# Feed-forward on one core: one pair of plain column blocks instead of two, and token sums formed just ahead of the block products that use them

## The chip, the cores and the metric

The kernel runs on one core of one Trainium2 chip. The metric is the device time of one launch in microseconds (us); of the kernel before three runs are shown, and their median is what the changed kernel is held against. The engines are named as in the profile: PE (TensorE, matmuls), PEld (its weight loads), DVE (VectorE), ACT (ScalarE), POOL (GpSimd), SP (SyncE, which here issues DMAs).

## The reference, cut to what matters

A trunk of two layers over 512 tokens of width 1024, in float32. Each layer has a feed-forward, a token mixer (layer 0: attention beside a gated delta rule; layer 1: a state-space scan) and another feed-forward, so there are four feed-forwards in all. The change touches these alone:

```
def swiglu(x, w_gate, w_up, w_down):
    return (jax.nn.silu(x @ w_gate) * (x @ w_up)) @ w_down
...
        f = swiglu(rmsnorm(h, nw[0]), ffn_w_gate[layer, 0], ffn_w_up[layer, 0], ffn_w_down[layer, 0])
        h = h + FFN_RES_SCALE * rmsnorm(f, nw[1])
```

`w_gate` and `w_up` are 1024 x 2816, that is 22 column blocks of 128.

## The kernel before, in words

**Float32 products as three matmuls.** Each operand is split into a high part `hi` (a cast on ACT, line 80) and a rest `lo` (a subtraction on DVE, line 81); a product is hi·hi + hi·lo + lo·hi. The normalised tokens stand transposed in two tiles `uhi` and `ulo` (together `uT`: 4 token blocks x 8 blocks of the contraction x 128). A unit of weights is 128 x 1024 numbers (512 KB): it is loaded into a raw tile (`wraw`, 3 buffers, or `wq`, 5 buffers) and split into `whi` and `wlo` (4 buffers each, for all of the kernel).

**The order of the columns in a feed-forward** (`ffn`, lines 304 to 438). Blocks are done in pairs.

1. Blocks 0 and 1 (`early`, lines 326 to 336): gate and up of both, four units, which hold all four `whi`/`wlo` buffers. Every product is done for token blocks 0 and 1 first, then for 2 and 3 (24 matmuls of 256 columns each time), since the last tokens come late from the stage before. Then `finish` (lines 320 to 323) takes SiLU of the gate on ACT and multiplies it with the up product on DVE into a tile `hT`.
2. Blocks 2 and 3 (`plain`, lines 338 to 344): four products of 24 matmuls over all 512 tokens.
3. Token sums (lines 347 to 370): with `uT` seen as a 2 x 2 matrix of quarters A11, A12 (first tokens) and A21, A22 (last tokens), the full-precision quarters r11, r12, r21, r22 are formed (hi + lo, line 352) and combined into S2, S1n, S3 and S4, each again split into hi and lo (`parts`). The r tiles are four of the eleven buffers that `place` gives out under the name `h`, and the `hT` tiles come from the same eleven. S4 is written over A21.
4. Blocks 4 to 21, nine pairs (lines 392 to 423): gate and up of a pair together take seven block products (`block_product`, line 293) of 24 matmuls with 256 columns, by Winograd's scheme: b11·A11, b21·A12, (t1 + b22)·S2, t1·S1n, t3·S3, b22·S4, (b11 + b21)·A22, the sums on the weights' side among them. A pair loads seven units: five by SP, and two more by POOL as loads that add into a `wq` tile already there (line 380: t1 and t3). The sum b11 = t1 + b22 (line 405) waits for the first of these and for b22.

Then `out_product` multiplies with `w_down` and applies the norms, the residual and the next norm (`finish` and `pre` there), and the transposed tokens of the next stage come out of it, token block by token block.

**What sets the order.** The text gives each instruction a priority, its place in the program. When the kernel is built, every engine gets one list: of what is ready by the builder's model of times, the earliest in the text goes first. On the chip each engine runs its list in that order. `self.tc.cur_priority` (lines 148 and 157) moves the transposes of the last tokens back by a count of instructions (`BEHIND`). Buffers of one name are given out in the order in which the text first writes them.

**A count that spans stages.** `weights` counts units in `n_weights` (line 93), and in the even mixer, where `share` is set, every fifth has its `lo` formed by POOL instead of DVE (line 94). A `w_cols` or `w_rows` unit counts, a `unit`/`forms` of the block pairs doesn't.

Of the kernel before, what the change touches and what calls it, by code (L numbers as in the profile page):

```python
# [14 lines left out]
OP = mybir.AluOpType  # L15
# [15 lines left out]
class Trunk:  # L31
# [272 lines left out]
    def ffn(self, w_gate, w_up, w_down, post_w, next_pre, raws={}):  # L304
# [3 lines left out]
        nf = w_gate.shape[1] // 128  # L308
        tt, stt = nc.vector.tensor_tensor, nc.vector.scalar_tensor_tensor
        with ExitStack() as ctx:  # L310
            hp = ctx.enter_context(self.tc.tile_pool(name="ffn_h", bufs=1, reuse_waits="tile"))

            place = lambda dt=F32: hp.tile([128, 2, T], dt, name="h", bufs=nf // 2)
            early, plain = 2, 2
            acc, wts, hT = {}, {}, []
            with ExitStack() as ctx2:
                pool = lambda name, **kw: ctx2.enter_context(self.tc.tile_pool(name=name, reuse_waits="tile", **kw))
# [2 lines left out]
                def finish(f):  # L320
                    s = self.scratch()
                    nc.scalar.activation(s, acc[f, 0], AF.Silu)
                    tt(hT[f // 2][:, f % 2, :], acc[f, 1], s, op=OP.mult)

                r11, r12, r21, r22 = (place().rearrange("p f (k c) -> p f k c", c=128) for _ in range(4))
                for f in range(early):
                    for g, w in ((0, w_gate), (1, w_up)):
                        wts[f, g] = self.w_cols(w, f * 128, raw=raws.get((f, g)))
                        acc[f, g] = self.ps("acc" if f else "mm")
                        self.product(acc[f, g][:, :256], wts[f, g], 0, 2)  # L330
                for f in range(early):
                    for g in range(2):
                        self.product(acc[f, g][:, 256:], wts[f, g], 2, 4)
                    if f == 0:
                        hT.append(place())
                    finish(f)

                for f in range(early, early + plain):
                    if f % 2 == 0:
                        hT.append(place())  # L340
                    for g, w in ((0, w_gate), (1, w_up)):
                        acc[f, g] = self.ps("mm")
                        self.product(acc[f, g], self.w_cols(w, f * 128))
                    finish(f)


                half = lambda i, j: [u[:, 2 * i:2 * i + 2, 4 * j:4 * j + 4, :] for u in self.uT]
                A11, A12, A21, A22 = (half(i, j) for i in range(2) for j in range(2))
                flat = lambda x: x.rearrange("p t k c -> p t (k c)")

                def whole(r, x):
                    tt(flat(r), flat(x[0]).bitcast(F32), flat(x[1]).bitcast(F32), op=OP.add)

                def parts(r, x):
                    self.split(flat(r), *(flat(y) for y in x))
                    return x

                new = lambda n: [sp.tile([128, 2, KD // 2, 128], F32R, name=n + x) for x in ("hi", "lo")]
                whole(r11, A11)
                whole(r21, A21)  # L360
                whole(r22, A22)
                tt(flat(r21), flat(r22), flat(r21), op=OP.subtract)
                stt(flat(r11), flat(r21), -1.0, flat(r11), op0=OP.mult, op1=OP.subtract)
                S2 = parts(r11, new("s2"))
                S1n = parts(r21, new("s1"))
                stt(flat(r22), flat(r11), -1.0, flat(r22), op0=OP.mult, op1=OP.subtract)
                S3 = parts(r22, new("s3"))
                whole(r12, A12)
                stt(flat(r12), flat(r11), -1.0, flat(r12), op0=OP.mult, op1=OP.subtract)
                S4 = parts(r12, A21)  # L370

                def unit(f, pool, name, *parts):

                    raw = pool.tile([128, KD // 2, 256], F32, name=name)
                    for i, (w, k) in enumerate(parts):
                        src = w[k * 128:(k + KD // 2) * 128, f * 128:(f + 2) * 128].rearrange("(k p) c -> p k c", p=128)
                        if i == 0:
                            nc.sync.dma_start(raw, src)
                        else:
                            nc.gpsimd.dma_start(raw, src, accum_op=OP.add)  # L380
                    return raw

                def forms(raw):
                    hi, lo = (self.wsplit.tile([128, KD // 2, 256], F32R, name=x) for x in ("whi", "wlo"))
                    self.split(raw, hi, lo)
                    return hi, lo
# [2 lines left out]
                q = lambda n: qp.tile([128, 512], F32, name=n)  # L389

                two = lambda x: x.rearrange("p (f t) -> p f t", f=2)
                for f in range(early + plain, nf, 2):
                    b11, b21 = unit(f, wq, "wq", (w_gate, 0)), unit(f, self.wraw, "wraw", (w_gate, 4))
                    t1 = unit(f, wq, "wq", (w_gate, 0), (w_up, 0))
                    b22 = unit(f, self.wraw, "wraw", (w_up, 4))
                    t3 = unit(f, wq, "wq", (w_up, 4), (w_up, 0))
                    a = self.ps("mm")
                    self.block_product(a, forms(b11), A11, True)
                    q1 = q("q1")
                    nc.scalar.copy(q1, a)  # L400
                    c = self.ps("acc")
                    self.block_product(c, forms(b21), A12, True)
                    add(q1, c, q1)
                    nc.scalar.activation(q1, q1, AF.Silu)
                    add(b11, t1, b22)
                    self.block_product(a, forms(b11), S2, False)
                    q2 = q("q2")
                    nc.scalar.copy(q2, a)
                    d = self.ps("acc")
                    self.block_product(d, forms(t1), S1n, True)  # L410
                    q3 = q("q3")
                    nc.scalar.copy(q3, d)
                    self.block_product(a, forms(t3), S3, False)
                    add(q3, a, q3)
                    self.block_product(d, forms(b22), S4, False)
                    add(q2, d, q2)
                    hT.append(place())
                    stt(hT[-1][:, :, :256], two(q2), -1.0, two(q1), op0=OP.mult, op1=OP.mult)
                    add(b21, b11, b21)
                    self.block_product(a, forms(b21), A22, False)  # L420
                    s = self.scratch()
                    nc.scalar.activation(s, a, AF.Silu)
                    stt(hT[-1][:, :, 256:], two(q3), -1.0, two(s), op0=OP.mult, op1=OP.mult)
# [778 lines left out]
```

## Time and profile before

| | us |
|---|---|
| Runs of the kernel before | 2155.16, 2157.08, 2158.19 |
| Their median | 2157.08 |
| The profiled execution, its own time | 2155.31 |
| Its span, first to last instruction | 2153.5 |
| PE busy in the span | 2112.7 |
| DVE busy in the span | 1479.1 |
| ACT busy in the span | 1026.2 |

Durations come from the one profiled execution, so a sum stands against its own time; 1.8 us of that lie outside the span. The granted clock of PE was 0.996 of its full 2.4 GHz as a mean over the span. The matmuls overlap one another, so that the distance from one start to the next, not the duration, says what a matmul takes.

### The profile page before, as it was taken

To read this page: it belongs to the slowest core of one execution; us is meant where nothing else is said; L and a number is where in the kernel's file an instruction comes from. 1 tells how busy PE (TensorE), PEld (TensorE's weight loads), DVE (VectorE), ACT (ScalarE), POOL (GpSimd) and SP (SyncE) were. 2 spreads that over 40 slices of the span, in tenths; PEclk is the share of its full clock that TensorE was granted. 3 is DMA by queue.
4 is the path that set the end of the run, shared out by engine and by line. 5 is a ranking of instruction groups with operands and counts; after the bars stand their busy time and mean duration, and the time that the engine had idled before them with its cause. 6 is when DMAs were issued, how large, how long until landed. Compare 5 with 4: busy or idle time off the path is not lost.

```text
span 2153.5 us, 33163 instructions
## 1 busy us (share of the span) xinstructions
PE 2112.7 (98%) x13311; PEld 1871.1 (87%) x13311; DVE 1479.1 (69%) x2329; ACT 1026.2 (48%) x1577; POOL 149.5 (7%) x142
## 2 busy tenths in 40 slices
PE   8999999999999999999999999999999999999998
PEld 7999988887788999988899998877778788999986
DVE  5866656869667767656686765668888846867653
ACT  4544543455563454534344455347565423544541
POOL 0011000111200011000001100000000000011000
PEclk9999999999999999999999999999999999999999
DMA  8687334342323687533658642324334236586321
GB/s 235 148 195 167 118 100 135 101 126 66 88 70 117 158 205 176 127 118 98 157 138 196 157 132 94 101 74 118 98 90 126 69 118 157 142 196 157 122 89 68
DMA packets 284037, 277.06 MB, mean 129 GB/s; under 512 B 18576, under 2 KB 244552, under 8 KB 283884
## 3 DMA queue, kind: packets, MB, share of 16 engines
q1 hardware_dynamic: 243308, 228.81, 35.0%
q0 software_dynamic: 40576, 46.14, 13.0%
q8 instruction: 104, 1.70, 0.3%
q14 instruction: 49, 0.40, 0.1%
HBM read 265.93 MB, written 4.79 MB: 126 GB/s over the span
## 4 chain that ended last, share of the span: by engine, by line
PE 84%; DVE 7%; DMA 4%; ACT 3%; issue 1%; SPq 0%; POOL 0%; DVEq 0%; ACTq 0%; POOLq 0%
PE mm L300 18%; PE acc L300 13%; PE acc L235 9%; PE acc L237 9%; PE acc L236 9%; PE mm L169 4%; PE mm L168 4%; PE mm L167 4%; DMA wraw<-in_ffn_w_up_dram 2%; DMA M<-rows_o 1%; PE acc L649 1%; DVE wlo L81 1%; PE tr L154 1%; PE acc L169 1%; PE acc L167 1%
## 5 line engine op out<-in xcount | busy, mean ns | idle before, releaser
L80 ACT CAST whi<-wraw 128x1024 fp32r<-128x1024 f32 x296 | 310.0, 1049 | 400.0 <-PE acc L237 107.4
L81 DVE TENSOR_TENSOR wlo<-wraw,whi 128x1024 fp32r<-128x1024 f32 x292 | 356.5, 1223 | 143.4 <-ACT whi L80 141.6
L167 PE MATMUL mm<-uhi,whi 128*128 128x512 f32 (+1 forms) x736 | 274.1, 373 | 1.6 <-DVE feat L476 1.3
L168 PE MATMUL mm<-ulo,whi 128*128 128x512 f32 (+1 forms) x736 | 272.9, 371 | 0.2 <-DVE ulo L81 0.2
L169 PE MATMUL mm<-uhi,wlo 128*128 128x512 f32 (+1 forms) x736 | 271.5, 369 | 0.0
L80 ACT CAST whi<-wq 128x1024 fp32r<-128x1024 f32 x144 | 150.8, 1049 | 241.4 <-issue 77.4
L81 DVE TENSOR_TENSOR wlo<-wq,whi 128x1024 fp32r<-128x1024 f32 x144 | 175.4, 1222 | 96.7 <-ACT whi L80 96.6
L235 PE MATMUL acc<-whi,hs 128*128 128x512 f32 x576 | 227.3, 395 | 0.0
L236 PE MATMUL acc<-wlo,hs 128*128 128x512 f32 x576 | 227.2, 394 | 0.0
L380 POOL DMA_DIRECT2D wq<-in_ffn_w_up_dram x72 | 92.7, 1290 | 1074.3 <-DMA wq<-in_ffn_w_gate_dram 404.0
L300 PE MATMUL mm<-uhi,whi 128*128 128x256 f32 x576 | 163.8, 284 | 3.2 <-DVE q L388 3.1
L300 PE MATMUL mm<-uhi,wlo 128*128 128x256 f32 x576 | 163.0, 283 | 0.0
L300 PE MATMUL mm<-ulo,whi 128*128 128x256 f32 x576 | 163.0, 283 | 0.0
L300 PE MATMUL acc<-uhi,whi 128*128 128x256 f32 x576 | 162.8, 283 | 0.0
L300 PE MATMUL acc<-uhi,wlo 128*128 128x256 f32 x576 | 162.8, 283 | 0.0
L300 PE MATMUL acc<-ulo,whi 128*128 128x256 f32 x576 | 162.8, 283 | 0.0
L167 PEld LDWEIGHTS mm<-uhi,whi 128*128 128x128 f32 x736 | 139.1, 189 | 26.3 <-issue 2.9
L168 PEld LDWEIGHTS mm<-ulo,whi 128*128 128x128 f32 x736 | 139.4, 189 | 25.2 <-issue 5.0
L169 PEld LDWEIGHTS mm<-uhi,wlo 128*128 128x128 f32 x736 | 139.4, 189 | 23.8 <-issue 3.6
L237 PE MATMUL acc<-whi,hs 128*128 128x512 f32 x384 | 151.5, 395 | 0.0
L236 PEld LDWEIGHTS acc<-wlo,hs 128*128 128x128 f32 x576 | 108.5, 188 | 25.3
L235 PEld LDWEIGHTS acc<-whi,hs 128*128 128x128 f32 x576 | 108.5, 188 | 25.0
(393 smaller groups left out, 5240.1 us busy)
## 6 DMA issues: line engine op xcount, KB each, us to landing
wraw<-in_ffn_w_down_dram SPq DMA_DIRECT2D x88, 512.0 KB, 3.5
wq<-in_ffn_w_gate_dram SPq DMA_DIRECT2D x72, 512.0 KB, 5.4
wq<-in_ffn_w_up_dram POOLq DMA_DIRECT2D x72, 512.0 KB, 7.6
wraw<-in_ffn_w_gate_dram SPq DMA_DIRECT2D x52, 512.0 KB, 5.4
wraw<-in_ffn_w_up_dram SPq DMA_DIRECT2D x52, 512.0 KB, 6.4
wraw<-in_odd_w_in_dram SPq DMA_DIRECT2D x40, 512.0 KB, 3.9
wq<-in_ffn_w_up_dram SPq DMA_DIRECT2D x36, 512.0 KB, 3.8
wraw<-in_even_w_in_dram SPq DMA_DIRECT2D x28, 512.0 KB, 4.3
```

Source lines behind the costliest of these rows:

```text
L80: nc.scalar.copy(hi, src)
L81: (nc.gpsimd if on_pool else nc.vector).tensor_tensor(lo, src, hi.bitcast(F32), op=OP.subtract)
L154: nc.tensor.transpose(p[:, j * 128:(j + 1) * 128], u[:, k * 128:(k + 1) * 128], self.ident)
L167: nc.tensor.matmul(p, whi[:, k, :], hi, start=k == 0, stop=False)
L168: nc.tensor.matmul(p, whi[:, k, :], lo, start=False, stop=False)
L169: nc.tensor.matmul(p, wlo[:, k, :], hi, start=False, stop=k == KD - 1)
L235: nc.tensor.matmul(p, ahi, hi, start=k == 0, stop=False)
L236: nc.tensor.matmul(p, ahi, lo, start=False, stop=False)
L237: nc.tensor.matmul(p, alo, hi, start=False, stop=k == nk - 1)
L300: self.nc.tensor.matmul(p[:, f * 256:(f + 1) * 256].rearrange("p (t c) -> p t c", c=128), l, r, start=new and f == k == i == 0, stop=f == ...
L380: nc.gpsimd.dma_start(raw, src, accum_op=OP.add)
L649: nc.tensor.matmul(p[:, c, :], lhs[:, c, :], rhs[:, c, :], start=True, stop=True)
```

## The change

The second plain pair (blocks 2 and 3) goes; its columns become a tenth block pair, at the front of the loop. The loop over block pairs starts right behind `early`. r11 and r12 are formed between the first and second halves of the early products. The other sums are formed in the first block pair, each by `token_sum(n)` behind the split of the weights and just ahead of the block product that takes it.

```diff
-            early, plain = 2, 2
+            early = 2
...
+                whole(r11, A11)
+                whole(r12, A12)
                 for f in range(early):
                     for g in range(2):
                         self.product(acc[f, g][:, 256:], wts[f, g], 2, 4)
...
-                for f in range(early, early + plain):
-                    if f % 2 == 0:
-                        hT.append(place())
-                    for g, w in ((0, w_gate), (1, w_up)):
-                        acc[f, g] = self.ps("mm")
-                        self.product(acc[f, g], self.w_cols(w, f * 128))
-                    finish(f)
...
-                whole(r11, A11)
-                whole(r21, A21)
-                whole(r22, A22)
-                tt(flat(r21), flat(r22), flat(r21), op=OP.subtract)
-                stt(flat(r11), flat(r21), -1.0, flat(r11), op0=OP.mult, op1=OP.subtract)
-                S2 = parts(r11, new("s2"))
-                S1n = parts(r21, new("s1"))
-                stt(flat(r22), flat(r11), -1.0, flat(r22), op0=OP.mult, op1=OP.subtract)
-                S3 = parts(r22, new("s3"))
-                whole(r12, A12)
-                stt(flat(r12), flat(r11), -1.0, flat(r12), op0=OP.mult, op1=OP.subtract)
-                S4 = parts(r12, A21)
+                sums = {}
+
+                def token_sum(n):
+
+                    if n in sums:
+                        return sums[n]
+                    if n == 2:
+                        whole(r21, A21)
+                        whole(r22, A22)
+                        tt(flat(r21), flat(r22), flat(r21), op=OP.subtract)
+                        stt(flat(r11), flat(r21), -1.0, flat(r11), op0=OP.mult, op1=OP.subtract)
+                        sums[n] = parts(r11, new("s2"))
+                    elif n == 1:
+                        sums[n] = parts(r21, new("s1"))
+                    elif n == 3:
+                        stt(flat(r22), flat(r11), -1.0, flat(r22), op0=OP.mult, op1=OP.subtract)
+                        sums[n] = parts(r22, new("s3"))
+                    else:
+                        stt(flat(r12), flat(r11), -1.0, flat(r12), op0=OP.mult, op1=OP.subtract)
+                        sums[n] = parts(r12, A21)
+                    return sums[n]
...
-                for f in range(early + plain, nf, 2):
+                for f in range(early, nf, 2):
...
-                    self.block_product(a, forms(b11), S2, False)
+                    wt, u = forms(b11), token_sum(2)
+                    self.block_product(a, wt, u, False)
...
-                    self.block_product(d, forms(t1), S1n, True)
+                    wt, u = forms(t1), token_sum(1)
+                    self.block_product(d, wt, u, True)
...
-                    self.block_product(a, forms(t3), S3, False)
+                    wt, u = forms(t3), token_sum(3)
+                    self.block_product(a, wt, u, False)
...
-                    self.block_product(d, forms(b22), S4, False)
+                    wt, u = forms(b22), token_sum(4)
+                    self.block_product(d, wt, u, False)
```

## Rows read from the trace of the kernel before

**Rows 1.** The page: busy time by engine, and the chain that ended last by engine

```profile
PE 2112.7 (98%) x13311; PEld 1871.1 (87%) x13311; DVE 1479.1 (69%) x2329; ACT 1026.2 (48%) x1577; POOL 149.5 (7%) x142
...
PE 84%; DVE 7%; DMA 4%; ACT 3%; issue 1%; SPq 0%; POOL 0%; DVEq 0%; ACTq 0%; POOLq 0%
```

**Rows 2.** Stretches: length, busy PE, PEld, DVE, ACT, POOL, granted clock, DMA, GB/s

```profile
41.55:63.34 21.79, 21.79 (x98) 18.03 (x97) 14.97 (x14) 7.19 (x8) 0.00 (x0) 1.00 0.34 91
63.34:243.80 180.46, 180.46 (x1513) 180.45 (x1512) 130.64 (x132) 93.39 (x113) 19.29 (x15) 1.00 0.69 167
700.98:712.48 11.50, 11.50 (x96) 11.31 (x95) 5.37 (x6) 5.73 (x7) 2.62 (x2) 1.00 0.93 233
...
1086.45:1270.70 184.25, 181.69 (x1513) 180.65 (x1512) 130.11 (x132) 93.28 (x113) 19.28 (x15) 1.00 0.68 163
```

**Rows 3.** The chain that ended last, two block pairs of the first feed-forward

```profile
80.67 5.76 PE mm L300 x48
...
100.72 5.76 PE mm L300 x48
```

**Rows 4.** DVE in order of time, first feed-forward, from the second halves to the sums

```profile
34.12 1.23 DVE L81 TENSOR_TENSOR wlo<-wraw,whi 128x1024 fp32r<-128x1024 f32 x1 [5.64 <-ACT whi L80]
36.05 0.69 DVE L323 TENSOR_TENSOR h<-mm,scr 128x512 f32<-128x512 f32 x1 [0.71 <-ACT scr L322]
...
42.25 0.69 DVE L323 TENSOR_TENSOR h<-acc,scr 128x512 f32<-128x512 f32 x1 [1.19 <-PE acc L169]
...
52.73 0.69 DVE L323 TENSOR_TENSOR h<-mm,scr 128x512 f32<-128x512 f32 x1 [2.17 <-PE mm L169]
53.34 4.62 DVE L352 TENSOR_TENSOR h<-uhi,ulo 128x1024 f32<-128x1024 f32 x4
```

**Rows 5.** DVE in order of time, second feed-forward

```profile
690.16 0.15 DVE L106 TENSOR_SCALAR rs_x<-ss_sum 128x1 f32<-128x1 f32 x1
690.22 1.22 DVE L81 TENSOR_TENSOR wlo<-wraw,whi 128x1024 fp32r<-128x1024 f32 x1
...
700.60 1.42 DVE L81 TENSOR_TENSOR ulo<-tr,uhi 128x512 fp32r<-128x512 f32 x2 [1.46 <-ACT uhi L80]
...
721.34 1.23 DVE L388 TENSOR_TENSOR wq<-wq,wraw 128x1024 f32<-128x1024 f32 x1 [1.11 <-DMA wraw<-in_ffn_w_up_dram]
723.66 0.69 DVE L323 TENSOR_TENSOR h<-mm,scr 128x512 f32<-128x512 f32 x1 [1.09 <-PE mm L169]
724.27 1.22 DVE L352 TENSOR_TENSOR h<-uhi,ulo 128x1024 f32<-128x1024 f32 x1
```

**Rows 6.** ACT in order of time, first feed-forward, the first cast behind the early units

```profile
33.04 1.05 ACT L80 CAST whi<-wraw 128x1024 fp32r<-128x1024 f32 x1 [5.32 <-PE mm L168]
```

**Rows 7.** Instruction groups: count, busy us, mean ns of one, idle time before

```profile
L81 DVE TENSOR_TENSOR wlo<-wraw,whi 128x1024 fp32r<-128x1024 f32 x292 | 356.5, 1223 | 143.4 <-ACT whi L80 141.6
...
L352 DVE TENSOR_TENSOR h<-uhi,ulo 128x1024 f32<-128x1024 f32 x16 | 18.5, 1218 | 0.0
...
L323 DVE TENSOR_TENSOR h<-mm,scr 128x512 f32<-128x512 f32 x12 | 8.3, 689 | 10.3 <-PE mm L169 8.2 <-ACT scr L322 2.1
...
L81 POOL TENSOR_TENSOR wlo<-wraw,whi 128x1024 fp32r<-128x1024 f32 x4 | 10.3, 2573 | 53.2 <-ACT whi L80 53.2
```

**Rows 8.** DVE in order of time, fourth feed-forward, the last tokens' rest

```profile
1807.51 1.37 DVE L81 TENSOR_TENSOR ulo<-tr,uhi 128x512 fp32r<-128x512 f32 x2 [2.82 <-ACT uhi L80]
```

**Rows 9.** POOL's adding loads: two of the second feed-forward, and line 380's time to landing

```profile
704.95 2.62 POOL L380 DMA_DIRECT2D wq<-in_ffn_w_up_dram  x2 [103.03 <-DMA wq<-in_ffn_w_gate_dram]
...
DMA to landing us min/median/max: 6.0/7.6/11.8
```

**Rows 10.** DVE's waits (total us, times, longest), and a load in the third feed-forward's chain

```profile
DVE wq L388 <- DMA wraw<-in_ffn_w_up_dram: 24.3, 17, 2.9
...
1114.72 8.44 DMA wraw<-in_ffn_w_up_dram
```

More of the change, by code (lines that the diff above doesn't have):

```diff
@@ L330, in ffn, with whole @@
                         self.product(acc[f, g][:, :256], wts[f, g], 0, 2)
+                half = lambda i, j: [u[:, 2 * i:2 * i + 2, 4 * j:4 * j + 4, :] for u in self.uT]
+                A11, A12, A21, A22 = (half(i, j) for i in range(2) for j in range(2))
+                flat = lambda x: x.rearrange("p t k c -> p t (k c)")
+                def whole(r, x):
+                    tt(flat(r), flat(x[0]).bitcast(F32), flat(x[1]).bitcast(F32), op=OP.add)
+                whole(r11, A11)
+                whole(r12, A12)
                 for f in range(early):
@@ L336, in ffn @@
                     finish(f)
-                for f in range(early, early + plain):
-                    if f % 2 == 0:
-                        hT.append(place())
-                    for g, w in ((0, w_gate), (1, w_up)):
-                        acc[f, g] = self.ps("mm")
-                        self.product(acc[f, g], self.w_cols(w, f * 128))
-                    finish(f)
[L347 to L352, printed above, removed]
                 def parts(r, x):
```

## The prediction

> **What bounds the kernel now.** I read the page first: PE is busy for 98% of the span and holds 84% of the chain that ended last [rows 1]. So time is saved where PE's work shrinks, and lost where PE comes to wait. The table of stretches says what each stage of a feed-forward costs [rows 2]: the plain pair 41.55 to 63.34, 21.79 us; the nine block pairs behind it 180.46 us. In the chain one pair follows the other after 100.72 - 80.67 = 20.05 us [rows 3], and 9 x 20.05 = 180.45, so the pairs run without a gap in the first feed-forward; in the third they took 184.25 us [rows 2]. The clock granted is 1.00 in all these stretches, the 2.4 GHz level, and nothing in the change lets PE rest long.
>
> Next I read DVE's list in order of time. In the first feed-forward it idles 5.64 us ahead of 34.12, and the four token sums stand at 53.34, right behind the product of line 323 at 52.73 that first writes the second hT tile [rows 4]; in the second feed-forward the same pair is at 723.66 and 724.27 [rows 5]. The sums read only tokens that the early second halves had read by 41.55 [rows 2], over 11 us before. I take it that the buffers of the name h go out in the text's order, so that r11 had to follow hT[1]. This says where they can stand after the change: r11 and r12 as soon as the tokens are there, r21 and r22 behind the line-323 product of block 0, which stands at 36.05 [rows 4].
>
> **The change, part by part.**
>
> *The pair.* A plain pair of 21.79 us becomes a block pair of 20.05: -1.74 us in each feed-forward, **-6.96** in four. (The Trainium skill, TensorE: Matmul & The Clock Gate, Back-to-back issue gap, gives N/2.4 + 2.5 ns for a matmul of N columns; by it 96 matmuls of 512 against 168 of 256 would differ by an estimated 2.4 us, 9.5 in all. The trace shows 21.79/96 = 227 ns and 20.05/168 = 119 ns, so the measurement decides.)
>
> *The first block pair's DVE work.* In order of need, all the times on the first feed-forward's scale. The second halves end at 41.55 and block products start every 20.05/7 = 2.86 us: product 3, which takes S2, at 47.3, product 5, which takes S3, at 53.0. DVE's first act is the rest of b11's split at 34.12: its cast at 33.04 waits for an early product to let go of a buffer [rows 6], and that stays. From there on a long operation (1.22 us by its row [rows 7]) takes 1.13 when it follows another, (4.62 - 1.22)/3 [rows 4], a short one (0.69 [rows 7]) 0.61 by the same overlap. Up to the rest of S2 DVE has ten long ones (b11, the sum t1 + b22, b21, r21, r22, b11 again, two combinations, t1, S2) and two short (line 323 twice): 11.3 + 1.2 = 12.5, done at 46.6, 0.7 us before product 3. Up to the rest of S3 there are six more long ones (S1, t3, b22, the combinations for S3 and for S4, S3; b22 and S4's slip in while ACT casts S3) and one short: 6.8 + 0.6, done at 54.0, 1.0 us behind product 5. So PE stalls **1.0** in each, 4.0 in all. Ends: 0 if b22 and the combination for S4 come later (2.3 us saved), 3.3 if two more long operations get ahead. Behind product 5 the next products' inputs are done in time, and S4 and the rest stay within PE's pace. ACT's casts fit in between (1.05 each [rows 6]).
>
> *r11 and r12 ahead of the second halves.* They come into the list while the last tokens are still being normed. Short dependent operations of that chain leave openings, and the builder puts long ones in: a weight's rest stands at 690.22 between two of them [rows 5]. In the second feed-forward the chain has no slack: the last tokens' rest runs from 700.60 to 702.02 [rows 5], and the second halves start at 700.98 [rows 2]. Two insertions delay it by 2.3, of which the 1.46 us of idle time just ahead of it [rows 5] can take up the most: 2.3 - 1.46 = 0.8, and I book **1.0** each for the second and the third, whose start looks alike. In the fourth DVE has 2.82 us idle ahead of that rest [rows 8], in the first 5.64 idle behind it [rows 4]: nothing. Sum 2.0; ends 0 and 4 x 2.3 = 9.2.
>
> *The late load of the second feed-forward.* POOL issues t1's second load at 704.95 and the fastest of these landed after 6.0 us [rows 9]: 710.95, where the second halves run from 700.98 to 712.48 [rows 2]. The sum b11 = t1 + b22 is placed early: the builder counts on faster loads than there are, for DVE waited 24.3 us in 17 places at this very sum [rows 10], as at 721.34, where the line-323 product stands behind it [rows 5]. With the plain pair gone, its wait holds up what is queued behind it on DVE: eight long and two short operations up to S2's rest. 710.95 + 9 x 1.13 + 1.2 = 722.3, and product 3 is due at 712.48 + 5.7 + 1.0 = 719.2: **3.1** in this feed-forward alone. Ends: 0 if the builder puts the sum later, 4.7 with the median landing of 7.6. (The Trainium skill, the same page, Architectural detail: the array is 16× 32×32, says that VectorE's queue is strictly first in, first out. The trace agrees: nothing passes the sum at 721.34. This rule speaks against the change.)
>
> *Loads.* A plain pair loads 4 units, a block pair 7, three more for SP and POOL, 12 in all. In these stretches the DMA engines are 0.34 busy against 0.69 in the pairs [rows 2], so there is room; four loads leave the `wraw` queue on SP and two join it, and b21 and b22 come earlier. In the third feed-forward b22's load sits in the chain for 8.44 us [rows 10], and nine pairs lost 184.25 - 180.46 = 3.8 us: one more pair there costs **0.4**. Ends 0 and 4 x 0.4.
>
> *Behind the first pair* there are as many hT tiles, DVE operations and PSUM banks a pair as before: nothing. *The count of units* falls by four before the even mixer, so that POOL's turn, 2.57 us against DVE's 1.22 [rows 7], falls on other weights, four either way: 0, ends -5.4 and +5.4, since nothing says whether the ones it leaves or the ones it takes matter more.
>
> The sum: -6.96 + 4.0 + 2.0 + 3.1 + 0.4 = +0.5, so 2155.8 against the profiled execution's own 2155.3. That one stands 1.8 below the median of the runs, so against the median it is **2157.6**: PE's gain is given back by waits on DVE in the first block pairs. 0.2%, or 4.3 us, is about what a measurement of this kernel tells from no change, so this is no change.
>
> **The rivals.**
>
> *The sums are hidden* (faster). If the list puts S3 ahead of b22, r11 and r12 into idle time, and the late sum behind the token sums, only the load of the third feed-forward is left: 2157.1 - 6.96 + 0.4 = 2150.5. For it speaks that 34.12 has 5.64 us of idle DVE ahead of it [rows 4], that S2 has 0.7 us of room and that S3 misses by one operation only; against it that in four feed-forwards all three places would have to come out well. It shows as faster while the waits stay under 2.7 us in all. 0.2.
>
> *The sums start late* (slower). If r21 and r22 come behind the second line-323 product (42.25 [rows 4]) and not the first (36.05), the S2 chain starts at 42.9: five long operations and a cast, 5 x 1.13 + 1.05 and some 0.1 of handing over, end at 49.7, 2.4 us late for product 3, with S3's 1.0 still behind it: 2.4 more in each than in my sum, 2157.6 + 9.6 = 2167. It decides from 0.7 us on, which is S2's room. For it: before, the sums stayed behind a product that they don't need; against it: they followed the first writer of an hT tile, and in the new text that is block 0's. 0.14.
>
> *Loads become the bound.* If all four feed-forwards lose what the third loses now, 3 x 3.8 = 11.4 more: 2169. For it: 8.44 us for one load [rows 10]; against: the first ran its nine pairs in 180.46 [rows 2]. 0.04.
>
> *The change doesn't do what it says*: the list stays as it was, since order is the builder's, and the sums wait as they did; then only the pair counts, and this is the hidden case's time. Within its 0.2.
>
> **How the numbers follow.** No change as summed 0.62, hidden 0.2, late sums 0.14, loads 0.04. From the first I give 0.04 to slower, for the upper ends of its terms (S3 at 3.3, the load at 4.7), and nothing to faster, which the hidden case holds: faster 0.2, same 0.58, slower 0.22. The likeliest is 2157.6. Its own range is 2153 to 2162. To leave out no more than 2 in 10 the range goes down to 2151, where half of the hidden case is in, and up to 2165, short of the late sums.
>
> **What would show it.** The pairs: ten a feed-forward, 20.05 us each from the second on, and no plain matmul of 512 columns behind the early products. PE's waits: one at the fifth product of the first pair, by the rest of S3, near 1 us in each feed-forward; one at product 3 of the second feed-forward, by a DVE operation that stands behind the sum b11, near 3 us; a later start of the second halves in the second and third by 1 us. I am wrong if r21 stands anywhere but behind block 0's line-323 product, if the first pair's DVE list has idle time ahead of S2, or if the time moves in a mixer: then the count of units did it.

## The result, and the profile after

| | before | after |
|---|---|---|
| median, us | 2156.2 (2155.2 to 2158.2, 5 runs) | 2171.3 (2167.7 to 2181.4, 5 runs) |
| ratio | 1 | 1.0068 [1.0047, 1.0089] |
| profiled execution: span, us | 2153.5 | 2179.6 |

The change costs 0.7%, where no change was forecast; the range ended at 2165. Two more runs of before came with the result, which is why their median is now 2156.2 and not 2157.08. The profiled execution of after is the longest of its five; a second profile of the same kernel, taken later as a yardstick, has a span of 2166.9 and stands beside it below.

The page of after, busy time and the chain by engine, to be read against [rows 1]:

```profile
PE 2118.9 (97%) x13599; PEld 1887.6 (87%) x13599; DVE 1507.0 (69%) x2361; ACT 1044.9 (48%) x1601; POOL 159.3 (7%) x150
...
PE 77%; DVE 9%; DMA 8%; ACT 4%; issue 2%; DVEq 0%; POOL 0%; SPq 0%; ACTq 0%; POOLq 0%
```

PE's share of the chain fell from 84% to 77%; DVE and DMA took it. Where, the stretches of after say (columns as in [rows 2]): in each feed-forward the first block pair, then the nine later ones.

```profile
41.03:62.41 21.38, 20.68 (x171) 20.24 (x170) 21.34 (x22) 12.69 (x15) 2.57 (x2) 1.00 0.69 164
62.41:246.15 183.74, 181.91 (x1514) 180.78 (x1513) 125.82 (x128) 92.52 (x113) 19.29 (x15) 1.00 0.70 167
714.51:743.79 29.28, 22.78 (x171) 22.08 (x170) 26.75 (x26) 13.12 (x16) 2.55 (x2) 0.88 0.66 140
743.79:929.50 185.71, 181.98 (x1514) 180.75 (x1513) 125.94 (x128) 92.66 (x113) 19.24 (x15) 1.00 0.68 164
1079.40:1101.18 21.78, 20.78 (x171) 20.29 (x170) 21.74 (x23) 12.61 (x15) 2.57 (x2) 1.00 0.59 148
1101.18:1286.20 185.02, 181.79 (x1515) 180.82 (x1514) 125.94 (x128) 92.53 (x113) 19.30 (x15) 1.00 0.70 165
1835.36:1862.29 26.93, 23.41 (x171) 22.80 (x170) 23.73 (x24) 12.28 (x15) 2.55 (x2) 0.87 0.62 134
1862.29:2048.95 186.66, 183.43 (x1514) 183.04 (x1513) 126.34 (x128) 92.70 (x113) 19.27 (x15) 0.98 0.68 163
```

A pair that waits for nothing takes 20.05 us [rows 3], nine take 180.45. So the four first pairs are 1.33, 9.23, 1.73 and 6.88 too long, **19.2** in all, and the later ones 3.3, 5.3, 4.6 and 6.2, **19.3** in all (before: 5.1, nearly all of it in the third and fourth). With the pairs' gain of -6.96 that is 19.2 + 19.3 - 5.1 - 6.96 = +26.4, and the spans differ by 26.1. What lies between the feed-forwards and at both ends adds up to nearly nothing (-0.3). The yardstick has 18.9 and 9.4: the first pairs' loss is steady, the later pairs' varies.

*The first pairs.* In the second feed-forward, VectorE's list in order of time, and behind it PE's (of PE five rows):

```profile
714.67 1.23 DVE L391 TENSOR_TENSOR wq<-wq,wraw 128x1024 f32<-128x1024 f32 x1 [3.08 <-DMA wq<-in_ffn_w_up_dram]
715.81 1.22 DVE L81 TENSOR_TENSOR wlo<-wraw,whi 128x1024 fp32r<-128x1024 f32 x1
716.95 1.22 DVE L337 TENSOR_TENSOR h<-uhi,ulo 128x1024 f32<-128x1024 f32 x1
718.08 0.69 DVE L323 TENSOR_TENSOR h<-acc,scr 128x512 f32<-128x512 f32 x1
718.68 1.22 DVE L81 TENSOR_TENSOR wlo<-wq,whi 128x1024 fp32r<-128x1024 f32 x1
719.82 1.22 DVE L337 TENSOR_TENSOR h<-uhi,ulo 128x1024 f32<-128x1024 f32 x1
720.95 1.22 DVE L81 TENSOR_TENSOR wlo<-wq,whi 128x1024 fp32r<-128x1024 f32 x1
722.09 1.22 DVE L362 TENSOR_TENSOR h<-h 128x1024 f32<-128x1024 f32 x1
723.22 1.22 DVE L81 TENSOR_TENSOR wlo<-wq,whi 128x1024 fp32r<-128x1024 f32 x1
724.36 0.69 DVE L391 TENSOR_TENSOR q<-acc,q 128x512 f32<-128x512 f32 x1
724.96 1.22 DVE L363 SCALAR_TENSOR_TENSOR h<-h 128x1024 f32<-128x1024 f32 x1
726.09 1.22 DVE L81 TENSOR_TENSOR s1lo<-h,s1hi 128x1024 fp32r<-128x1024 f32 x1
727.23 1.22 DVE L368 SCALAR_TENSOR_TENSOR h<-h 128x1024 f32<-128x1024 f32 x1
728.36 1.22 DVE L81 TENSOR_TENSOR s2lo<-h,s2hi 128x1024 fp32r<-128x1024 f32 x1
```

```profile
720.15 0.28 PE L300 MATMUL acc<-uhi,wlo 128*128 128x256 f32 x1
724.44 0.58 PE L300 MATMUL acc<-s1hi,whi 128*128 128x256 f32 x1 [4.01 <-ACT s1hi L80]
727.31 0.58 PE L300 MATMUL mm<-s2hi,whi 128*128 128x256 f32 x1 [2.28 <-ACT s2hi L80]
...
728.33 0.41 PE L300 MATMUL acc<-s1lo,whi 128*128 128x256 f32 x1
728.54 0.41 PE L300 MATMUL acc<-s1hi,wlo 128*128 128x256 f32 x1
```

From 714.67 on VectorE has no pause. The weight splits of b11, t1 and t3 stand among the four steps (two L337, L362, L363) that lead to S1 and S2, so the last of these ends at 726.18, and the builder has put the products with S1 and S2 into one another. PE is through its second product at 720.3 and waits 4.01 for S1 and 2.28 for S2. From this sum to S2's rest the fourth feed-forward has the same list, without the wait for t1 ahead of it; there PE waits 0.8 for S1 and 2.5 for S2. The matmuls after the pause are 0.21 us apart (728.33 to 728.54) where those ahead of it were 0.12: the stretches give the granted clock as 1.00 up to the wait, 0.51 behind it, the lower level of 1.2 GHz; from 731.30 to 743.79 it is 1.00 again.

```profile
700.00:718.83 18.83, 18.83 (x156) 18.40 (x156) 10.81 (x13) 8.49 (x10) 3.87 (x3) 1.00 0.88 196
724.44:731.30 6.86, 4.58 (x20) 4.28 (x21) 6.86 (x8) 3.52 (x4) 1.27 (x1) 0.51 0.78 176
```

Twenty matmuls at 0.21 in place of 0.12 add some 1.9 us to the waits of 6.3.

*The later pairs.* The chain in a later pair of the first feed-forward:

```profile
150.88 1.24 DVE wlo L81
...
152.14 7.40 DMA wraw<-in_ffn_w_up_dram
...
160.80 0.70 DVE q L391
...
161.54 4.46 PE mm L300 x35
```

The split at 150.88 lets a `wraw` buffer go; b22's load for the next pair goes out at once, takes 7.40 us, and VectorE, which comes to the sum b11 = t1 + b22 before that, holds the add into q3 behind it, for which PE's seventh product waits. The waits of the whole run, PE's first, then VectorE's:

```profile
PE mm L300 <- DVE q L391: 12.0, 14, 3.2
...
PE acc L300 <- ACT s1hi L80: 4.9, 2, 4.0
PE mm L300 <- ACT s2hi L80: 4.8, 2, 2.5
```

```profile
DVE wq L391 <- DMA wraw<-in_ffn_w_up_dram: 48.8, 27, 4.8
```

In [rows 10] VectorE's wait at this sum was 24.3 us in 17 places. The median landing of these loads rose from 6.4 to 7.0 us.

### The profile page after: what moved, and what is told of

Same layout as the page of the kernel before. It is cut to its first block, busy times and chain, and to the rows that moved or that the text cites. A ratio compares the mean times of both kernels' runs of the same rounds, so it can differ in the third digit from the quotient of the medians.

```text
span 2179.6 us, 33823 instructions
## 1 busy us (share of the span) xinstructions
PE 2118.9 (97%) x13599; PEld 1887.6 (87%) x13599; DVE 1507.0 (69%) x2361; ACT 1044.9 (48%) x1601; POOL 159.3 (7%) x150
## 4 chain that ended last, share of the span: by engine, by line
PE 77%; DVE 9%; DMA 8%; ACT 4%; issue 2%; DVEq 0%; POOL 0%; SPq 0%; ACTq 0%; POOLq 0%
PE mm L300 17%; PE acc L300 11%; PE acc L235 9%; PE acc L236 9%; PE acc L237 9%; DMA wraw<-in_ffn_w_up_dram 5%; PE mm L168 3%; PE mm L169 3%; PE mm L167 3%; DVE wlo L81 2%; DMA M<-rows_o 1%; PE acc L656 1%; ACT whi L80 1%; PE tr L154 1%; PE acc L1079 1%
## 5 line engine op out<-in xcount | busy, mean ns | idle before, releaser
L81 DVE TENSOR_TENSOR wlo<-wq,whi 128x1024 fp32r<-128x1024 f32 x160 | 194.8, 1221 | 96.1 <-ACT whi L80 96.0
L167 PE MATMUL mm<-uhi,whi 128*128 128x512 f32 (+1 forms) x608 | 223.9, 369 | 2.0 <-DVE feat L483 1.7
L168 PE MATMUL mm<-ulo,whi 128*128 128x512 f32 (+1 forms) x608 | 224.4, 369 | 0.2 <-DVE ulo L81 0.2
L169 PE MATMUL mm<-uhi,wlo 128*128 128x512 f32 (+1 forms) x608 | 221.3, 364 | 0.0
L300 PE MATMUL mm<-uhi,whi 128*128 128x256 f32 x640 | 184.4, 288 | 12.0 <-DVE q L391 12.0
L300 PE MATMUL mm<-uhi,wlo 128*128 128x256 f32 x640 | 182.1, 285 | 0.0
L300 PE MATMUL mm<-ulo,whi 128*128 128x256 f32 x640 | 182.1, 285 | 0.0
L300 PEld LDWEIGHTS mm<-uhi,whi 128*128 128x128 f32 x640 | 123.8, 194 | 15.7 <-DVE q L391 15.5
L168 PEld LDWEIGHTS mm<-ulo,whi 128*128 128x128 f32 x608 | 115.4, 190 | 21.8 <-issue 5.7
L167 PEld LDWEIGHTS mm<-uhi,whi 128*128 128x128 f32 x608 | 114.9, 189 | 21.5 <-issue 3.2
L169 PEld LDWEIGHTS mm<-uhi,wlo 128*128 128x128 f32 x608 | 115.4, 190 | 18.3 <-issue 3.4
```

Source lines behind the costliest of these rows:

```text
L81: (nc.gpsimd if on_pool else nc.vector).tensor_tensor(lo, src, hi.bitcast(F32), op=OP.subtract)
L167: nc.tensor.matmul(p, whi[:, k, :], hi, start=k == 0, stop=False)
L168: nc.tensor.matmul(p, whi[:, k, :], lo, start=False, stop=False)
L169: nc.tensor.matmul(p, wlo[:, k, :], hi, start=False, stop=k == KD - 1)
L300: self.nc.tensor.matmul(p[:, f * 256:(f + 1) * 256].rearrange("p (t c) -> p t c", c=128), l, r, start=new and f == k == i == 0, stop=f == ...
```

## The experiments

Two things were to be told apart: the sums of u late in the first pair, and b22 late in the later ones; and for each, whether it comes from the pair taken away, from the new place of the sums, or from the three units more that a block pair loads. The table holds all runs. "First" and "later" are what the four first pairs and the later pairs took beyond 20.05 us each in the profile, from the starts of PE's products.

| kernel | median, us | ratio to before | first | later |
|---|---|---|---|---|
| kept | 2151.5 | 0.9995 [0.9983, 1.0007] | 0.0 | 0.3 |
| block | 2169.1 | 1.0075 [1.0059, 1.0091] | 27.5 | 2.3 |
| early_sums | 2143.6 | 0.9958 [0.9943, 0.9974] | 2.1 | 2.6 |
| own_b22 | 2153.3 | 0.9994 [0.9982, 1.0005] | 13.0 | 0.1 |
| after_again | 2168.9 | 1.0069 [1.0048, 1.0089] | 18.9 | 9.4 |
| pool_sum | 2159.8 | 1.0037 [1.0022, 1.0052] | 21.6 | 1.0 |
| early_pool | 2151.0 | 0.9990 [0.9977, 1.0003] | 4.2 | 3.4 |
| r_back | 2164.0 | 1.0054 [1.0033, 1.0074] | 16.8 | 6.8 |
| t1_first | 2222.1 | 1.0321 [1.0303, 1.0339] | 14.9 | 67.4 |
| early_own | 2141.5 | 0.9938 [0.9925, 0.9950] | 2.0 | 0.1 |
| early_sums_again | 2146.1 | 0.9961 [0.9949, 0.9974] | 2.0 | 3.5 |
| own_b22_again | 2152.8 | 0.9998 [0.9984, 1.0012] | 12.4 | 0.1 |

Four kernels at a time, in the table's order, ran on one chip with the same runs of before, whose medians were 2153.4, 2151.6 and 2152.8 us.

**kept**: the second plain pair back, the sums where the change puts them.

```diff
-            early = 2
+            early, plain = 2, 2
...
+                for f in range(early, early + plain):
+                    ...
-                for f in range(early, nf, 2):
+                for f in range(early + plain, nf, 2):
```

> The second plain pair is put back; the sums still stand one by one just ahead of the block products. Theory (the sums lost the plain pair's 20 us of cover, and VectorE, with the sums and the weight splits of the first block pair in one list, is late with S1 and S2): with the cover back the waits of the first block pairs (14.4 us over the four feed-forwards in the changed kernel's profile) go, and the time is that of the kernel before, 2154 to 2160. Rival (the order just ahead of the products is itself what loses): the first block pairs keep their waits and the time stays at 2164 to 2175.

0.9995, and a later stretch as in [rows 2], with no wait:

```profile
736.79:917.25 180.46, 180.46 (x1513) 180.46 (x1512) 130.21 (x131) 94.13 (x114) 19.23 (x15) 1.00 0.68 167
```

So the new place of the sums costs nothing while a plain pair covers them. The theory held, with a time 2.5 us below its range.

**block**: one plain pair, the sums in one block ahead of the block pairs.

```diff
+                for n in (2, 1, 3, 4):
+                    token_sum(n)
                 for f in range(early, nf, 2):
```

> One plain pair, as in the changed kernel, but all sums of u stand in one block ahead of the block pairs, as in the kernel before. Rival (the order just ahead is what loses): the loss goes and the pair's gain of 6.96 stays: 2149 to 2155. Theory (the cover is what is missing, whatever the order): the sums now precede the weight splits of the first pair, so the wait moves from S1 and S2 to the splits of the second and third product, and the time stays at 2162 to 2174.

1.0075: the wait moved, as the theory had it. PE's longest wait is now for a weight split that stands behind the sums:

```profile
PE mm L300 <- DVE wlo L81: 14.0, 3, 4.8
```

The first pairs lose even more than in after. Neither of these two orders helps where the 20 us of cover are missing: some 14 us of sums and combinations (twelve operations of 1.13) and as much of the pair's own work go through one in-order list. The later pairs, though, lose 2.3 in all, nearly all of it in the second feed-forward. The nine later pairs of the first, with seven units a pair, the shared buffers and first pairs that end late:

```profile
65.32:245.80 180.48, 180.48 (x1514) 180.48 (x1513) 126.23 (x127) 92.29 (x113) 19.28 (x15) 1.00 0.70 170
```

**early_sums**: the sums for S2 and S1 stand ahead of the second halves (and so do the functions that form them).

```diff
                 whole(r12, A12)
+                token_sum(2)
+                token_sum(1)
                 for f in range(early):
                     for g in range(2):
                         self.product(acc[f, g][:, 256:], wts[f, g], 2, 4)
```

> The changed kernel with the sums that make S2 and S1 moved up in the program, ahead of the second halves of the early pair, so that VectorE can form them there, where it idles; nothing else. Theory (sums late in the first pair): the PE waits for s1hi and s2hi go, 6.9 us in the second and 3.8 in the fourth feed-forward; of the 14.4 us of first-pair waits 2 to 5 stay, and the time is 2158 to 2165. Rival (the loads of blocks that come late are nearly all of the loss): 2167 to 2173, no change.

0.9958, better than the theory's 2158 to 2165. The first pairs' loss fell from the yardstick's 18.9 to 2.1; that is what the edit shows. The later pairs lose 2.6 where the yardstick loses 9.4, though nothing was done to a load, but this can't be put down to first pairs that end on time: block, on the same chip and with 27.5 lost in its first pairs, loses as little. From the third pair on VectorE writes and reads the same tiles in the same order in before, after, block and this run, so the difference lies in when the loads land (median 5.4 us in block and 5.2 here, against 7.0 in after and 6.7 in the yardstick). The changed kernel itself was not run on this chip; whether chip or timing makes its loads late stays open.

**own_b22**: b22 in two buffers of its own; no more bytes are loaded.

```diff
-                wq, sp, qp = pool("ffn_w", bufs=5), ...
+                wq, wb, sp, qp = pool("ffn_w", bufs=5), pool("ffn_b", bufs=2), ...
...
-                    b22 = unit(f, self.wraw, "wraw", (w_up, 4))
+                    b22 = unit(f, wb, "wb", (w_up, 4))
```

> The changed kernel with block b22 in a pool of its own, two buffers of 4 KB, so that its load need not wait for b21's buffer to come free; the bytes loaded are the same. Theory (a late b22 holds the sum b11' on VectorE, which runs in order, and the add into q3 behind it holds the seventh product): VectorE's waits for loads in the sums, 48.8 us in the profile of after, fall below 20; the PE waits for them in the later pairs, 14.6 us in the profile, go, the runs come closer together than 14 us, and the time is 2162 to 2168 with the first-pair waits left. Rival (the transfers themselves cannot keep up with one pair of blocks more): the loads only start earlier and last longer, and the time stays at 2168 to 2176.

0.9994: a gain larger than the theory's, since VectorE waits for none of these loads any more (1.1 us is left at this sum, for t1's load) and the first pairs lost less too (13.0). The load is issued in the same place of a pair as before, but now for the pair after the next: from the n-th load's issue to the n-th sum it is 25.8 us in the later pairs, where it was 7 to 8 in after, the wait included. These loads' time to landing:

```profile
DMA to landing us min/median/max: 4.2/5.4/14.2
```

Neither the slowest, 14.2 us ahead of the first pair, nor the slowest among the pairs, 9.3 us from 70.61 on, was waited for. The transfers keep up; the rival falls.

**after_again**: the changed kernel, unaltered, as yardstick.

> The changed kernel itself, unaltered, on the chip of the other runs of this call, as the yardstick for them. b22's load landed in 7.0 us (median) in the profile of the changed kernel and in 4.7 to 5.4 us in the four experiments so far, and it has about 5.7 us before VectorE wants it. Theory (first-pair waits make up the steady part of the loss, late loads of b22 the varying part): with loads that land in 5 us the first-pair waits stay (some 14 us over the four) and the time is 2160 to 2168; with 7 us it is 2168 to 2180. Rival (the late loads are the change's own doing, three units more per pair): the median landing is 6.8 us or more again, and 2168 to 2180.

1.0069, as in the first measurement; a median landing of 6.7 us, and VectorE waited 39.8 us for b22. That is close to the theory's case of 7 us; the rival's landing of 6.8 is nearly met too, so this run alone doesn't tell them apart, own_b22 does.

**pool_sum**: b11 summed on GpSimd.

```diff
-                    add(b11, t1, b22)
+                    nc.gpsimd.tensor_tensor(b11, t1, b22, op=OP.add)
```

> The changed kernel with the sum b11' = t1 + b22 on GpSimd in place of VectorE; the rest of VectorE's list stays as it is. Theory (a late b22 or t1 blocks VectorE, which runs in order, and the add into q3 behind the sum is what PE waits for): PE's waits for q (12.0 us in the changed kernel's profile) fall below 2; the sum costs GpSimd about 2.4 us (as its 128x1024 splits) and the loads that GpSimd issues come that much later; the first-pair waits mostly stay; 5 to 10 us below the changed kernel on the same chip. Rival (late loads hurt whichever engine waits, since the third product needs the sum anyway): the PE waits move to the splits of b11' and the time is within 3 us of the changed kernel.

9.1 us below the yardstick. PE's waits for VectorE's q are gone though b22 landed in 7.7 us (median); 2.2 us for ACT's copy of q1 came in, and the sum took 2.65 us there (mean). The later pairs lose 1.0 where they lost 9.4, on the same chip. So it is VectorE's order that turns a late load into a late product. Of the profiles' 9.8 us, 8.4 are the later pairs and 3.5 the odd mixer (last section), less 2.7 that the first pairs lose more. These waits stay:

```profile
PE acc L300 <- ACT s1hi L80: 5.5, 2, 4.7
PE mm L300 <- ACT s2hi L80: 3.6, 2, 1.9
```

**early_pool**: both edits, early_sums and pool_sum.

> Both together: the sums for S2 and S1 ahead of the second halves of the early pair, and b11' summed on GpSimd. Theory: the two losses are separate and both go: under 3 us of PE waits are left in the block pairs, and the time is 2138 to 2144, below the kernel before by 9 to 16. Rival (the first experiment with early sums had already nothing left to gain, its late loads having gone with the waits): 2143 to 2147, as that one.

A miss: 0.9990, above early_sums by 0.3%. With little late there was little to save, and something new came in: the first pairs lose 4.2, the second pairs of two feed-forwards 3.2, where PE waits for ACT's copy of q1 (L405). In that of the second feed-forward the trace shows why: GpSimd's sum stands behind its own issue of a load, for which it waited 7.55 us, and ends at 735.7; ACT idles 7.12 us for it, has three casts and a SiLU to do, and comes to the copy at 739.08 (rows of GpSimd, ACT and PE):

```profile
732.01 1.27 POOL L385 DMA_DIRECT2D wq<-in_ffn_w_up_dram  x1 [7.55 <-DMA wq<-in_ffn_w_gate_dram]
732.79 2.93 POOL L410 TENSOR_TENSOR wq<-wq,wraw 128x1024 f32<-128x1024 f32 x1
735.75 2.00 ACT L80 CAST whi<-wq 128x1024 fp32r<-128x1024 f32 x2 [7.12 <-POOL wq L410]
...
739.08 0.58 ACT L405 COPY q<-mm 128x512 f32<-128x512 f32 x1
739.72 0.39 PE L300 MATMUL mm<-s2hi,whi 128*128 128x256 f32 x1 [1.14 <-ACT q L405]
```

So the late load now holds other in-order lists, those of GpSimd and ACT. 4.0 of the profiles' difference from early_sums lie in the odd mixer (last section).

**r_back**: r11 and r12 back to where they are used.

```diff
-                whole(r11, A11)
-                whole(r12, A12)
...
                     if n == 2:
+                        whole(r11, A11)
...
                     else:
+                        whole(r12, A12)
```

> The changed kernel with the sums r11 and r12 moved back, from ahead of the second halves to the places at products 3 and 6 where they are used. The prediction held that their early place delays the last tokens by 1.0 us in two feed-forwards (2.0 in all). By it the time falls by 2 there, but VectorE's first-pair list grows by one or two adds of 1.14 us, so S2 comes 1.1 later in each: 2 to 5 us slower than the changed kernel on the same chip. Rival (their early place costs something in the mixers after all, beyond the sight of the stage table): 2 to 6 us faster.

5 us faster than the yardstick, so neither was right: the rival had the size and not the place. The first pairs of the first and third feed-forward lose 1.8 more each, as an S2 that comes later would have it, but those of the second and fourth 4.1 and 1.6 less, for the builder made another list of them. The stage ahead of the second feed-forward's pairs is 0.8 longer than in the yardstick, that of the third's 0.2 shorter, so the early place costs the last tokens nothing. Of the profiles' 6.7 us, 2.7 are the odd mixer's again, 2.2 the first pairs' and 2.6 the later ones'; the first of these comes and goes with no edit.

**t1_first**: one line moved, no bytes more.

```diff
+                    t1 = unit(f, wq, "wq", (w_gate, 0), (w_up, 0))
                     b11, b21 = unit(f, wq, "wq", (w_gate, 0)), ...
-                    t1 = unit(f, wq, "wq", (w_gate, 0), (w_up, 0))
                     b22 = unit(f, self.wraw, "wraw", (w_up, 4))
```

> The changed kernel with one line moved: the two loads that sum to t1 stand ahead of b11's and b21's, so that t1 takes the buffer that comes free first. The prediction put 3.1 us (0 to 4.7) on a late t1 in the second feed-forward; in the changed kernel VectorE waited there 3.1 to 4.0 us for it with the whole list of sums behind, and the first block pair took 9.2 to 10.1 us too long. Theory (that wait is passed on to S1 and S2 one for one): the wait goes, the second feed-forward's first pair falls to 5 to 7 us too long, as the fourth's, and the time falls by 3 to 5, to 1.0045 to 1.0055 of before. Rival (the list is full anyway, so t1's wait is hidden in it): no change, 1.0065 to 1.0072.

3.2% slower, the clearest of all. VectorE's wait for t1 is gone and the second feed-forward's first pair fell from the yardstick's 10.1 to 8.1, so at most 2 us hung on it there; the fourth's, which had no such wait, fell as much (5.8 to 3.7), so even these 2 are not shown to be the wait's. But t1's first load is now the first of the two `wq` loads from w_gate, GpSimd issues the second at 808.80, 0.65 us ahead of b22's at 809.45 (in after it went out 3.8 us behind it, 155.98 against 152.14), and b22's load takes 9.00 us. A later pair of the second feed-forward in the chain, and the waits of the run:

```profile
808.20 1.24 DVE wlo L81
...
809.45 9.00 DMA wraw<-in_ffn_w_up_dram
...
819.71 0.70 DVE q L391
```

```profile
PE mm L300 <- DVE q L391: 45.8, 27, 3.3
```

The median landing is 8.2 us, with the same bytes. (The Trainium skill, DMA: Bandwidth & Descriptors, Issuing engines are not separate DMA queues, says that transfers started by different engines run on the same 16 DMA engines and interleave; these rows agree, at 9.00 us against 7.40.)

**early_own**: early_sums and own_b22 together.

> Both repairs that paid best together: the sums for S2 and S1 ahead of the second halves, and b22 in buffers of its own. In the profile with the early sums alone 2.1 us were left in the first pairs and 2.6 in the later ones. Theory (the first-pair list and the late b22 are separate terms): the later pairs' 2.6 goes, the time is 1 to 3 us below that of the early sums alone on the same chip, 0.994 to 0.996 of before. Rival (with the first pairs in time the later pairs hold their phase by themselves): the same as the early sums alone, within 1 us.

0.9938, 11.3 us below before and 4.6 below early_sums on the same chip, where the theory had 1 to 3: the best of all. The first two feed-forwards, ten pairs each, which without any wait would take 200.5 (the third and fourth are as these, 200.60 and 201.60):

```profile
41.39:241.95 200.56, 200.56 (x1683) 200.56 (x1682) 145.34 (x146) 104.33 (x126) 21.85 (x17) 1.00 0.68 165
709.10:910.70 201.60, 200.87 (x1683) 200.67 (x1682) 147.20 (x149) 104.92 (x127) 21.79 (x17) 1.00 0.69 166
```

The waits were separate terms, as the theory had it: only 1.0 is left in two first pairs, and the later pairs lose 0.1 where early_sums_again loses 3.5. Of the gain, 11.3, the pairs' 6.96 and what before lost at late loads, 5.1 in its profile, less the 2.1 left, make 10.0.

**early_sums_again** and **own_b22_again**, beside it on the same chip.

> The kernel with the early sums once more, beside its combination with b22's own buffers and on a third draw of chip. Theory: 0.9945 to 0.997 of before again, with at most 3 us of waits in the first pairs, whatever b22's landing. Rival (the first result was luck of the chip, whose loads landed in 5.2 us): with landings near 7 us the later pairs lose 5 to 15 us and the ratio is 0.999 to 1.004.

> The kernel with b22 in buffers of its own once more, now beside the others on one chip: in its first run the later pairs lost 0.1 us in all, but on a chip where loads landed early. Theory (late landings of b22 feed on themselves through the shared buffers: a late sum makes VectorE late, which frees the buffers late, which starts the next loads late and closer together): with its own buffers the later pairs lose under 2 us whatever the landing, and the ratio is 0.999 to 1.001 again. Rival (it was the chip): the later pairs lose 5 to 15 us and the ratio is 1.003 to 1.007.

Both came out as the theories had them, with median landings of b22 of 5.4 us in each. A median near 7 us came with neither, so the rivals' case was not met as a whole; of single loads among the pairs one took 8.9 us in own_b22_again (from 743.40 on), and VectorE waited for none of b22's. In early_sums_again the first feed-forward's first pair is on time and its third still loses 1.5. With buffers of its own the chain of own_b22_again holds nothing but PE in a later pair:

```profile
134.53 2.85 PE mm L300 x24
137.38 2.87 PE acc L300 x24
140.25 5.76 PE mm L300 x48
```

## Why the prediction was wrong, by its steps

*The sum* was added up wrongly: -6.96 + 4.0 + 2.0 + 3.1 + 0.4 is +2.5 and not +0.5; the 2.0 of r11 and r12 is missing from it. By its own terms the forecast was 2159.6, still within its range. That those 2.0 did not come either, so that leaving them out did no harm, is luck.

*The pair, -6.96*: right. In early_own all ten pairs of the first feed-forward take 200.56. (The Trainium skill, TensorE: Matmul & The Clock Gate, Back-to-back issue gap, gives the formula that stood beside this term for an isolated matmul and not for a stream; the sum did not use it.)

*S3 late by 1.0 in each first pair, 4.0*: right in the first and third feed-forward (1.33 and 1.73; in both PE stops twice at the fifth product, 0.37 + 0.76 and 0.72 + 0.71, first until ACT has copied the third product, line 412, then until S3's rest is done). **This step failed in the second and fourth**: "in order of need, all the times on the first feed-forward's scale" took one list for all four. There the builder's list is another. From the sum b11 to S2's rest VectorE has twelve long operations in place of nine: t3's split, S1's rest and S3's combination came in (714.59 + 12 x 1.13 + 1.2 = 729.4; the rest ends at 729.58). PE waits 6.3 us for S1 and S2, and its granted clock is 0.51 behind the wait. 9.23 and 6.88 were lost where 1.0 + 3.1 and 1.0 stood. Together with the next term but one, 7.1 was booked for the first pairs and 19.2 measured; this alone would have made 2157.6 + 12.1 = 2170 (2157.6 holds the 7.1, and not the 2.0). In place of that step stands: the builder made another list for these two feed-forwards, and in it S1 and S2 come late (6.3 and 3.3 us of waits) and not S3.

*r11 and r12, 2.0*: wrong in place. The last tokens come no later: the time from the end of one feed-forward's pairs to the start of the next one's is 468.35 and 149.88 us, against 490.45 - 21.79 = 468.66 and 171.52 - 21.79 = 149.73 before. What r_back shows is that their place changes the list of the first pairs.

*The late t1, 3.1*: the wait is there, 3.08 us. The load went out at 707.05 and took 7.54 us, near the median of 7.6 [rows 9] that the prediction kept for its upper end, where it reckoned with the fastest, 6.0. What it cost PE is not shown: without it that pair took 2.0 us less (t1_first), but so did the fourth feed-forward's. It is at most a part of the 9 to 10 us and not their core.

*Loads, 0.4*: **the second step that failed.** "So there is room" went by the mean share of the DMA engines, 0.34 where the plain pair stood. The share in the later pairs is the same after as before (0.68 to 0.70 against 0.68 to 0.69 [rows 2]); what counts is one load and its time. In kept, where VectorE waits at 4 of 36 sums, b22 is issued 5.75 us ahead of its sum and lands in 4.7 (medians); before it landed in 6.4 and VectorE waited at 17 of 36, in after in 7.0 and at 27 of 40. The later pairs lost 0.3, 5.1 and 19.3 (the yardstick 9.4), where 0.4 was booked on top of before's. Shown is that b22 issued a pair earlier ends it (own_b22, twice, and early_own), that it is far worse where one more transfer runs beside it (t1_first), and that it hurts by VectorE's order (pool_sum). What makes the loads of after later than those of block, which loads as much a pair, is not shown; first pairs that end on time are not it. That it feeds itself, a late sum making VectorE late, so that buffers come free late and the next loads crowd together, fits the traces (in the sixth pair of the first feed-forward GpSimd's load of t3 goes out 0.43 us ahead of the third product in after, in the pair of the same columns in kept 1.93 ahead) but no run tested that alone.

*The count of units, 0*: right; the even mixer's stage is as long as before.

Of the rivals, *sums start late* had the kind of cause, S1 and S2 behind other work, but its place was r21 behind the second product of line 323. In the second feed-forward r21 stands between the two, and r22 behind both. *Loads become the bound* had the time, 2169, and was given 0.04; but own_b22 loads the same bytes without a wait for b22, so a buffer and not the transfers was short.

## What to carry to other kernels

Work that is taken off PE may have been the cover of work on an in-order engine: before it goes, write that engine's list for each place where the code runs, since the scheduler may order every one differently, and move what can be done early ahead of the gap (1.0068 became 0.9958 by moving two lines). A load with a few us of slack is a risk even where the DMA engines have room on average: see which buffer's release starts it, and give it a second one if SBUF has the space. Either of two separate repairs alone brought the changed kernel to the time of before or below it (0.9994 and 0.9958); both together made the change pay: 0.9938. And add up a forecast's terms a second time: here one of five was left out.

## What the runs showed that was not expected

The cost of PE's waits of 4.0 and 2.3 us was not 6.3 us: the twenty matmuls behind them ran at the 1.2 GHz level, granted clock 0.51 in that stretch, and added some 1.9. (The Trainium skill, TensorE: Matmul & The Clock Gate, Loop structure matters more than you think, has a wait of PE followed by a halved clock in its example; the rows agree.)

One line moved, with the same bytes loaded in another order and into other buffers, cost 2.5% (t1_first against the yardstick, 1.0321 against 1.0069).

In the odd mixer PE waits once for VectorE's M tile, 3.4 us in the profile of before and 4.4 in that of after; early_sums showed 0.5 and the same kernel run again 3.7 (0.5 to 0.9 in four of the runs, 3.4 to 4.4 in the others). So it comes and goes between runs of one kernel, and differences of 3 to 4 us between single profiles mean nothing until that stage's own rows are compared.
